# A low-rank gate product run unsplit in four column groups of the array, and a gate product over 128 rows

## The chip, the cores and the metric

The kernel runs on one core of one Trainium2 chip. The metric is device time in microseconds (us) from one execution of the whole program. The core has five engines with an instruction queue each: TensorE (PE in the profile, with its weight loads as PEld), VectorE (DVE), ScalarE (ACT), GpSimd (POOL) and SyncE (SP), which only issues transfers here. Sixteen DMA engines move the data.

## The reference

A two-layer decoder trunk over 256 positions of width 2048. Layer 0 has sliding-window attention heads beside gated linear attention heads; layer 1 has a state-space part beside another gated recurrence. The lines that matter are those of the decay gate of layer 0:

```python
def ab_layer(h, w_in, gla_w_gate, gla_b_gate, gla_norm_g, w_out):      # h is rmsnorm(x) * norm_g
    z = h @ w_in
    qa, ka, va, qb, kb, vb, g_low, gate = jnp.split(z, AB_SPLIT, axis=-1)
    ...
    log_a = jax.nn.log_sigmoid(g_low @ gla_w_gate + gla_b_gate) / GLA_TAU
    ob = chunked_gated_linear_attention(qb * GLA_DK ** -0.5, kb, vb, log_a)
```

`g_low` has 16 columns (the low-rank product, 2048 to 16), and `gla_w_gate` takes these 16 to 512 (the gate product). Inputs and outputs are float32.

## The kernel before, in words

Activations lie feature-major: `hT` holds the input as 16 tiles (`KT`, index `kt`) of 128 features by 256 positions. The norm's factor per position is applied after a product (`rb0`, the same row on all partitions), and its gain per feature (`col(V_NG0 + kt)`) before it, in `split_x`. To keep float32 accuracy at the faster float32r format, the large products are split: `xh` and `xl` are the high and low part of the activations, `wh` (ScalarE, line 168) and `wl` (VectorE, line 169) those of a weight block, and three products are added (lines 181 and 200). Weight blocks come as 1 MB loads `raw` into three buffers, issued on SP (`load_split`). Small products run unsplit in float32.

The order of work: the instructions of an engine run in the order that a planner writes down when the program is built. It takes them by the order of the code, with a model of its own of what an instruction costs and when a result is there; blocks under `urgent()` go first, `issue_after` holds instructions behind a given one, and `hook` inserts prepared pieces between matmuls. Tiles with the same `tag` share a buffer.

What the change touches stands in `trunk`:

- `load_consts`, called with the fourth weight load of the first product, loads constants through SP. `wgt` is the gate weight, 16 rows of 512, loaded twice so that 32 partitions are filled (line 226).
- Lines 368 and 369 split the low-rank weight `glw` (128 by 16 by 16) into `glhl`: its high part in columns 0 to 15, its low part in 16 to 31.
- Lines 370 to 373: for each of the 16 `kt`, the 32 columns of `glhl` times `xh`, and the 16 high columns times `xl`, all into rows 0 to 31 of one PSUM tile `psl`. Rows 0 to 15 end up with the high part's product and rows 16 to 31 with the low part's.
- Line 374 multiplies by `rb0` into `glo`, 32 rows of 256.
- Line 379: four unsplit products of `wgt` (32 rows, 128 columns at a time) with `glo`. The sum over 32 rows adds the two halves. Lines 382 to 387 make the decay `f` from it, which `gla` (line 276) uses later.

Around it stand the transposed norm factor (line 127, just ahead in TensorE's order) and the second weight block's product (line 181). `s5_prep` builds tables for layer 1 from the start on; its transposes at line 935, the transfers of `ed` and `E` and its VectorE work run beside layer 0. `small_blocks` (line 287) and line 308 are unsplit products of 32 and 64 columns inside `gla`, line 504 transposes by a product with the identity, and line 272 clears `AT` (gA in the profile) on GpSimd.

Of the kernel before, what the change touches and what calls it, by code (L numbers as in the profile page):

```python
# [12 lines left out]
F32 = mybir.dt.float32  # L13
F32R = mybir.dt.float32r
I32 = mybir.dt.int32
AF = mybir.ActivationFunctionType
# [4 lines left out]
S = 256  # L21
D = 2048
KT = D // 128
# [4 lines left out]
V_NG0, V_NG1, V_FG, V_BG, V_GN, V_GAM, V_HN, V_BGLU = 0, 16, 32, 48, 52, 60, 76, 84  # L28
# [29 lines left out]
def trunk(ctx: ExitStack, tc: tile.TileContext, I, out):  # L58
    nc = tc.nc
    V, G, A, T = nc.vector, nc.gpsimd, nc.scalar, nc.tensor  # L60
# [16 lines left out]
    hT = xv[:, NV:].rearrange("p (k s) -> p k s", s=S)  # L77
    xh = const.tile([128, KT, S], F32R, name="xh")
    xl = const.tile([128, KT, S], F32R, name="xl")
# [7 lines left out]
    def col(o, n=1):  # L87
        return vec[:, o:o + n]

    def pm_tile(name="pm"):  # L90
        return pm.tile([128, 512], F32, name=name, tag="pm")
# [21 lines left out]
    def finish_norm(tag):  # L113
        V.tensor_add(sqa[:, 0:2], sqa[:, 0:2], sqa[:, 2:4])
        V.tensor_add(sqa[:, 0], sqa[:, 0], sqa[:, 1])
        ps = pm_tile()
        for t in range(2):
            T.matmul(ps[:, t:t + 1], sqa[:, 0, t * 128:(t + 1) * 128], ones[:, 0:1], start=True, stop=True)
        ms = small.tile([128, 2], F32, name="nms")
        V.tensor_scalar(ms, ps[:, 0:2], 1.0 / D, EPS, op0=OP.mult, op1=OP.add)  # L120
        rc = const.tile([128, 2], F32, name=tag + "c")
        rsqrt(rc, ms, 2, "nr")
        pb = pm_tile()
        for t in range(2):
            dg = small.tile([128, 128], F32, name="dg")
            V.tensor_scalar(dg, ident, rc[:, t:t + 1], None, op0=OP.mult)
            T.matmul(pb[:, t * 128:(t + 1) * 128], ones, dg, start=True, stop=True)
        rb = const.tile([128, S], F32, name=tag + "b")
        A.activation(rb, pb[:, 0:S], AF.Copy)
        return rc, rb  # L130
# [12 lines left out]
    def load_split(src, g):  # L143
        raw = stream.tile([128, 4, 512], F32, name="raw", bufs=3)
        first = state["first"]
        state["first"] = first and g < 3
        with urgent():
            if first:
                for a, b in ((0, 1), (1, 2), (2, 3), (3, 4)) if g == 0 else ((0, 2), (2, 4)):
                    xs = slice(NV + (4 * g + a) * S if g + a else 0, NV + (4 * g + b) * S)  # L150
                    load(xv[:, xs], I["xv"][:, xs])
                    for c in (slice(0, 256), slice(256, 512)) if g + a == 0 else (slice(0, 512),):
                        load(raw[:, a:b, c], src[g][:, a:b, c])
                for kt in range(4 * g, 4 * g + 4):
                    split_x(kt, V_NG0)
            else:
                state["load"] = nc.sync.dma_start(raw, src[g])
        if first and g == 3:
            load_consts()
        for half in range(2):  # L160
            wh = stream.tile([128, 2, 512], F32R, name="wh", bufs=3)
            wl = stream.tile([128, 2, 512], F32R, name="wl", bufs=3)
            with urgent():
                for a, b, c, d in (((0, 1, 0, 256), (0, 1, 256, 512), (1, 2, 0, 512)) if first and g == 0
                                   else ((0, 2, 0, 512),)):
                    r = raw[:, 2 * half + a:2 * half + b, c:d]
                    w, l = wh[:, a:b, c:d], wl[:, a:b, c:d]
                    state["wh"] = A.activation(w, r, AF.Copy)  # L168
                    V.tensor_sub(l, r, w)  # L169
            for k in range(2):  # L170
                yield 4 * g + 2 * half + k, wh[:, k], wl[:, k]
            hook()
# [42 lines left out]
    att = ExitStack()  # L215
    ap_ = att.enter_context(tc.tile_pool(name="att", bufs=1))
    glw = mix.tile([128, KT, 16], F32, name="glw", tag="gT1")
    glhl = ap_.tile([128, KT, 32], F32R, name="glhl", tag="pr")
    wgt = ap_.tile([32, 512], F32, name="wgt", tag="qk", bufs=2)
    glo = ap_.tile([32, S], F32, name="glo", tag="qk", bufs=2)  # L220

    def load_consts():
        nc.sync.dma_start(cst, I["cst"])
        nc.sync.dma_start(glw, I["w_low"])
        for n in range(2):
            nc.sync.dma_start(wgt[16 * n:16 * n + 16], I["w_gate"])
        nc.sync.dma_start(msk.rearrange("p a b -> p (a b)"), I["msk"])

    def load(dst, src):
# [16 lines left out]
    rc0, rb0 = finish_norm("r0")  # L246
# [118 lines left out]
            for t in range(2):  # L365
                A.activation(dst[:, t, c0:c0 + 512], ps[:, t], AF.Copy, scale=rc[:, t:t + 1])

    A.activation(glhl[:, :, 0:16], glw, AF.Copy)
    V.tensor_sub(glhl[:, :, 16:32], glw, glhl[:, :, 0:16])
    psl = pm_tile()  # L370
    for kt in range(KT):
        T.matmul(psl[0:32, 0:S], glhl[:, kt], xh[:, kt], start=(kt == 0), stop=False, skip_group_check=True)
        T.matmul(psl[0:16, 0:S], glhl[:, kt, 0:16], xl[:, kt], start=False, stop=(kt == KT - 1), skip_group_check=True)
    V.tensor_mul(glo, psl[0:32, 0:S], rb0[0:32])
    ga = mix.tile([128, 4, S], F32, name="gQ")
    for h0 in range(0, 4, 2):
        ps = pm_tile().rearrange("p (n s) -> p n s", n=2)
# [741 lines left out]
def build(arrays):  # L1119
    nc = bacc.Bacc("TRN2", target_bir_lowering=False, num_devices=1)  # L1120
    I = {k: nc.dram_tensor("in_" + k + "_dram", v.shape, mybir.dt.from_np(v.dtype), kind="ExternalInput").ap()
         for k, v in arrays.items()}
    out = nc.dram_tensor("out_0_dram", (2, 128, D), F32, kind="ExternalOutput").ap()
    with tile.TileContext(nc, schedule_with_timeline_sim=True) as tc:
        trunk(tc, I, out)
    if not nc.is_finalized():
        nc.finalize()
    return nc
# [8 lines left out]
```

## Time and profile before

| | |
|---|---|
| time, median of 3 runs | 893.63 us (893.55 to 894.71) |
| the profiled execution | 892.18 us, span 890.4 us |
| TensorE matmul busy | 874.7 us, 98% |
| VectorE busy | 635.5 us, 71% |
| ScalarE busy | 472.0 us, 53% |
| GpSimd busy | 54.4 us, 6% |
| mean transfer rate | 203 GB/s |
| granted TensorE clock, mean | 0.995 of full speed |

The span is what the profile covers of that execution; its own time is a little longer. Busy times of engines overlap. A row of the timeline or of a tile's view gives start, length, line, operation, the tiles written and read, the shape, and the count.

### The profile page before, as it was taken

To read this page: it belongs to the slowest core of one execution; us is meant where nothing else is said; L and a number is where in the kernel's file an instruction comes from. 1 tells how busy PE (TensorE), PEld (TensorE's weight loads), DVE (VectorE), ACT (ScalarE), POOL (GpSimd) and SP (SyncE) were. 2 spreads that over 40 slices of the span, in tenths; PEclk is the share of its full clock that TensorE was granted. 3 is DMA by queue.
4 is the path that set the end of the run, shared out by engine and by line. 5 is a ranking of instruction groups with operands and counts; after the bars stand their busy time and mean duration, and the time that the engine had idled before them with its cause. 6 is when DMAs were issued, how large, how long until landed. Compare 5 with 4: busy or idle time off the path is not lost.

```text
span 890.4 us, 18689 instructions
## 1 busy us (share of the span) xinstructions
PE 874.7 (98%) x7728; PEld 802.0 (90%) x7728; DVE 635.5 (71%) x1197; ACT 472.0 (53%) x715; POOL 54.4 (6%) x106
## 2 busy tenths in 40 slices
PE   8999999999999999999999999999999999999995
PEld 8987899889998899999999998799877899988894
DVE  7988975989869858756675677676987756665562
ACT  7654546665645765645543335355545475444451
POOL 0001100111101101000000001100110000000000
PEclk9999999999999999999999999999999999999998
DMA  9827743777656555555576566744643544544532
GB/s 317 316 102 218 259 160 146 237 256 251 220 204 230 205 190 196 197 200 199 200 283 222 206 230 198 260 172 167 225 166 139 206 190 172 202 180 177 179 132 94
DMA packets 40388, 180.40 MB, mean 203 GB/s; under 512 B 12720, under 2 KB 14256, under 8 KB 22768
## 3 DMA queue, kind: packets, MB, share of 16 engines
q1 hardware_dynamic: 29440, 154.99, 49.2%
q0 software_dynamic: 7984, 22.69, 7.5%
q10 hardware_dynamic: 2880, 1.54, 0.6%
q8 instruction: 60, 0.98, 0.4%
q14 instruction: 24, 0.20, 0.1%
HBM read 166.48 MB, written 12.71 MB: 201 GB/s over the span
## 4 chain that ended last, share of the span: by engine, by line
PE 81%; DVE 6%; DMA 4%; ACT 4%; issue 3%; SPq 0%; POOL 0%; ACTq 0%; POOLq 0%; DVEq 0%
PE pg L181 47%; PE pg L200 24%; DMA raw<-in_w_dram 2%; PE pg L756 2%; DVE wl L169 2%; PE pm L287 1%; PE pm L339 1%; DMA E<-ed 1%; ACT wh L168 1%; PE pm L621 1%; PE pm L625 1%; PE pm L308 1%; PE pm L415 1%; PE pm L1025 1%; ACT bb L1019 0%
## 5 line engine op out<-in xcount | busy, mean ns | idle before, releaser
L168 ACT ACTIVATE wh<-raw 128x1024 fp32r<-128x1024 f32 (+2 forms) x276 | 287.7, 1046 | 325.4 <-PE pg L181 193.7
L169 DVE TENSOR_TENSOR wl<-raw,wh 128x1024 fp32r<-128x1024 f32 (+2 forms) x276 | 332.0, 1206 | 167.9 <-ACT wh L168 163.1
L181 PE MATMUL pg<-xh,wh 128*128 128x256 f32 x1024 | 161.8, 279 | 2.2 <-ACT wh L168 2.2
L181 PE MATMUL pg<-xh,wl 128*128 128x256 f32 x1024 | 163.2, 280 | 0.4 <-DVE wl L169 0.4
L181 PE MATMUL pg<-xl,wh 128*128 128x256 f32 x1024 | 161.2, 278 | 0.0
L181 PEld LDWEIGHTS pg<-xh,wh 128*128 128x128 f32 x1024 | 136.7, 188 | 3.8 <-ACT wh L168 3.2
L181 PEld LDWEIGHTS pg<-xh,wl 128*128 128x128 f32 x1024 | 137.0, 188 | 1.6 <-DVE wl L169 0.8
L181 PEld LDWEIGHTS pg<-xl,wh 128*128 128x128 f32 x1024 | 136.7, 188 | 0.6 <-issue 0.3
L200 PE MATMUL pg<-wl,xh 128*128 128x512 f32 x320 | 100.9, 396 | 0.6 <-DVE wl L169 0.6
L200 PE MATMUL pg<-wh,xl 128*128 128x512 f32 x320 | 100.7, 394 | 0.0
L200 PE MATMUL pg<-wh,xh 128*128 128x512 f32 x320 | 100.2, 394 | 0.0
L200 PEld LDWEIGHTS pg<-wl,xh 128*128 128x128 f32 x320 | 59.0, 188 | 14.2 <-DVE wl L169 1.4
L200 PEld LDWEIGHTS pg<-wh,xl 128*128 128x128 f32 x320 | 59.8, 188 | 12.8
L200 PEld LDWEIGHTS pg<-wh,xh 128*128 128x128 f32 x320 | 59.3, 188 | 12.8
L181 PE MATMUL pg<-yh,wh 128*128 128x256 f32 x320 | 50.0, 277 | 0.0
L181 PE MATMUL pg<-yl,wh 128*128 128x256 f32 x320 | 49.5, 277 | 0.0
L181 PE MATMUL pg<-yh,wl 128*128 128x256 f32 x320 | 49.5, 277 | 0.0
L181 PEld LDWEIGHTS pg<-yh,wh 128*128 128x128 f32 x320 | 42.6, 188 | 0.0
L181 PEld LDWEIGHTS pg<-yl,wh 128*128 128x128 f32 x320 | 42.4, 188 | 0.0
L181 PEld LDWEIGHTS pg<-yh,wl 128*128 128x128 f32 x320 | 42.4, 188 | 0.0
L965 POOL DMA_DIRECT2D tabs<-pc x44 | 23.8, 547 | 162.3 <-DVE x L975 42.5
L200 PE MATMUL pg<-wh,yh 128*128 128x512 f32 x96 | 30.1, 395 | 0.0
(350 smaller groups left out, 1008.2 us busy)
## 6 DMA issues: line engine op xcount, KB each, us to landing
raw<-in_w_dram SPq DMA_DIRECT2D x100, 1024.0 KB, 4.9
raw<-in_wo_dram SPq DMA_DIRECT2D x28, 1024.0 KB, 4.8
tb<-tabs POOLq DMA_DIRECT2D x8, 768.0 KB, 6.9
tabs<-pc POOLq DMA_DIRECT2D x20, 256.0 KB, 5.5
raw<-in_wg_dram SPq DMA_DIRECT2D x4, 1024.0 KB, 4.8
raw<-in_wo1l_dram SPq DMA_DIRECT2D x4, 1024.0 KB, 4.8
raw<-in_w_dram SPq DMA_DIRECT2D x6, 512.0 KB, 7.9
tabs<-pc POOLq DMA_DIRECT2D x24, 128.0 KB, 4.6
```

Source lines behind the costliest of these rows:

```text
L168: state["wh"] = A.activation(w, r, AF.Copy)
L169: V.tensor_sub(l, r, w)
L181: state["mm"] = T.matmul(ps[:, c], w[:, cs], a[:, kt], start=(i == 0 and n == 0 and c % 2 == 0), stop=(i == last and n == 2), skip_group_c ...
L200: state["mm"] = T.matmul(ps[:, t], a[:, kt, ts_], w, start=(i == 0 and n == 0), stop=(i == last and n == 2), skip_group_check=True)
L287: T.matmul(ps[32 * b:32 * b + 32, t, hd], k[:, hd, r], Q[:, hd, r], start=True, stop=True)
L308: T.matmul(ps[j0:j0 + h, hd, j0 + h:j0 + 2 * h], k[:, hd, b:b + h], Qp[:, hd, b + h:b + 2 * h], start=True, stop=True)
L339: T.matmul(ps[:, (hd - h0) * dv:(hd - h0 + 1) * dv], AT[:, hd, t + j], v[:, j, hd * dv:(hd + 1) * dv], start=(j == 0), stop=(j == t))
L415: T.matmul(ps[:, t, 0:n], q[:, t * 128:(t + 1) * 128], k[:, 0:n], start=True, stop=True)
L621: T.matmul(py[g * 64:g * 64 + 64, pr], w[:, pr], X[:, g, pr], start=(pr == 0), stop=False, skip_group_check=True)
L625: T.matmul(py[gs, pr, 1:64], Pi[gs, pr], t["t"][1][gs, pr, 0:63], start=False, stop=True, skip_group_check=True)
L756: T.matmul(ps[:, t, 0:256], a_[:, kt, ts_], w_, start=(kt == 0 and n == 0), stop=(kt == KT - 1 and n == 2), skip_group_check=True)
L965: nc.gpsimd.dma_start(tabs[qt, dst, n], t[src].rearrange("p a b -> p (a b)"))
```

## The change

The low-rank weight is no longer split. It is multiplied by the norm's gain on VectorE into `glg`, whose columns 16 to 31 are zero (cleared on GpSimd), and multiplied unsplit with `hT` itself. The 16 products go in turn to the four 32-column groups of the array: `kt` 0, 4, 8, 12 add up in rows 0 to 31 of `psl`, `kt` 1, 5, 9, 13 in rows 32 to 63, and so on. Line 374 then spans 128 rows, and the gate product runs over 128 rows, with the gate weight repeated eight times down the partitions, so that its sum adds the four partial products (the rows that belong to the zero columns are zero). The repeated weight comes in one transfer that GpSimd issues, in place of two that SP issued.

```diff
-    glhl = ap_.tile([128, KT, 32], F32R, name="glhl", tag="pr")
-    wgt = ap_.tile([32, 512], F32, name="wgt", tag="qk", bufs=2)
-    glo = ap_.tile([32, S], F32, name="glo", tag="qk", bufs=2)
+    glg = ap_.tile([128, KT, 32], F32, name="glg", tag="pr")
+    wgt = ap_.tile([128, 512], F32, name="wgt", tag="qk", bufs=2)
+    glo = ap_.tile([128, S], F32, name="glo", tag="qk", bufs=2)
...
-        for n in range(2):
-            nc.sync.dma_start(wgt[16 * n:16 * n + 16], I["w_gate"])
+        wg_ = I["w_gate"]
+        nc.gpsimd.dma_start(wgt, bass.AP(tensor=wg_.tensor, offset=wg_.offset, ap=[[0, 8], [512, 16], [1, 512]]))
...
-    A.activation(glhl[:, :, 0:16], glw, AF.Copy)
-    V.tensor_sub(glhl[:, :, 16:32], glw, glhl[:, :, 0:16])
+    G.memset(glg, 0.0)
+    V.tensor_mul(glg[:, :, 0:16], glw, col(V_NG0, KT).unsqueeze(2).to_broadcast([128, KT, 16]))
     psl = pm_tile()
     for kt in range(KT):
-        T.matmul(psl[0:32, 0:S], glhl[:, kt], xh[:, kt], start=(kt == 0), stop=False, skip_group_check=True)
-        T.matmul(psl[0:16, 0:S], glhl[:, kt, 0:16], xl[:, kt], start=False, stop=(kt == KT - 1), skip_group_check=True)
-    V.tensor_mul(glo, psl[0:32, 0:S], rb0[0:32])
+        p = 32 * (kt % 4)
+        T.matmul(psl[p:p + 32, 0:S], glg[:, kt], hT[:, kt], start=(kt < 4), stop=(kt >= KT - 4),
+                 skip_group_check=True)
+    V.tensor_mul(glo, psl[:, 0:S], rb0)
```

## The prediction

> **What bounds the kernel now.** I read four views, in this order: the page's engine shares, what TensorE waited for, the chain that ended last in order of time, and the timeline of TensorE around the lines that change.
>
> ```profile
> span 890.4 us, 18689 instructions
> PE 874.7 (98%) x7728; PEld 802.0 (90%) x7728; DVE 635.5 (71%) x1197; ACT 472.0 (53%) x715; POOL 54.4 (6%) x106
> ```
> ```profile
> PE pg L181 <- ACT wh L168: 2.2, 3, 0.9
> ```
> TensorE (PE) is the bound: 98% busy, and the longest entry of its waits, 2.2 us in three waits, lies in the first 13 us. So 1 us taken out of TensorE's instruction stream should be close to 1 us of the span, as long as what feeds it moves along. The chain, read around the lines of the diff, says the same:
>
> ```profile
> 48.26 0.44 PE pm L127 x4
> 48.70 0.12 PE pm L372
> ...
> 52.35 0.12 PE pm L373
> ...
> 55.29 1.92 PE pm L379 x8
> ...
> 71.38 0.11 PE pm L935
> ```
> The low-rank product (L372 and L373, 16 each) and the gate product (L379) lie on the chain with their whole length. After L935 the chain leaves TensorE for the state-space preparation, but that starts with the transposes at L935, which stand behind all this in TensorE's order; if TensorE arrives there earlier, the transfers and VectorE work behind it start earlier too. I therefore let the full saving pass.
>
> **The change part by part.** First, prices of TensorE work, from the timeline (start, length, line, shape, count; starts are what I use, since the ends overlap).
>
> ```profile
> 48.10 0.60 PE L127 MATMUL pm<-dg,ones 128*128 128x128 f32 x4
> 52.30 0.40 PE L181 MATMUL pg<-xl,wh 128*128 128x256 f32 x2
> 54.42 0.64 PE L181 MATMUL pg<-xh,wh 128*128 128x256 f32 x4
> 54.90 0.40 PE L181 MATMUL pg<-xl,wh 128*128 128x256 f32 x2
> 55.22 1.99 PE L379 MATMUL pm<-glo,wgt 32*128 32x256 f32 x8
> 57.14 0.51 PE L181 MATMUL pg<-xl,wh 128*128 128x256 f32 x2
> 57.49 0.62 PE L181 MATMUL pg<-xh,wl 128*128 128x256 f32 x4
> 121.09 0.28 PE L181 MATMUL pg<-xh,wl 128*128 128x256 f32 x1
> 121.30 0.76 PE L287 MATMUL pm<-gQ,gk 128*32 128x32 f32 x64
> 121.99 0.62 PE L181 MATMUL pg<-xh,wl 128*128 128x256 f32 x3
> 122.45 0.62 PE L181 MATMUL pg<-xh,wh 128*128 128x256 f32 x4
> 136.65 0.28 PE L181 MATMUL pg<-xh,wh 128*128 128x256 f32 x1
> 136.85 1.15 PE L308 MATMUL pm<-gQ,gk 128*64 128x64 f32 x16
> 137.93 0.62 PE L181 MATMUL pg<-xh,wh 128*128 128x256 f32 x3
> 741.48 1.91 PE L504 MATMUL pm<-cst,gz 128*128 128x128 f32 x16
> 743.14 0.72 PE L181 MATMUL pg<-xh,wh 128*128 128x256 f32 x4
> ```
> What the reader is to see: an unsplit float32 matmul shows as two records (L379 issues 4 in the code and has 8 here), a split one (float32r) as one. A float32 record of 128 columns takes (743.14 - 741.48)/16 = 0.104 us, so one of 256 columns about 0.21 us, near the 0.24 us of L379, which includes a changeover. A split record of 256 columns at L181 takes (54.90 - 54.42)/4 = 0.12 us.
>
> (1) Old low-rank product. L127's four records start at 48.10 and need 4 x 0.107, so the product begins at 48.53; the next L181 starts at 52.30. It costs 3.77 us for 32 records.
>
> (2) New low-rank product: 16 unsplit matmuls of 256 columns, 32 records. One after the other that is 32 x 0.214 = 6.85 us, more than before. All depends on whether four column groups run at once. L287 has the same form: 128 rows, 32 columns, unsplit, four neighbouring matmuls into the four 32-partition strips of one tile. From the end of the L181 before (121.09 + 0.114) to the next L181 is 0.79 us; the three L181 after it take 0.46 instead of 0.34, so it costs 0.91 us in all for 64 records. Serially, 64 records of 32 columns would need 64 x 0.104/4 = 1.66 us. So they overlap; with four at a time the records need 16 rounds of 0.026 to 0.032, or 0.42 to 0.51, and the other 0.40 to 0.49 is the changeover into and out of the narrow shape. The 64-column L308, 16 records on one strip and so serial, costs 137.93 - 136.76 + 0.12 = 1.29 us, of which 16 x 0.052 to 0.058 is work: again about 0.4 for the changeover. New price: 8 rounds x 0.214 + 0.40 = 2.11 us. Saving 3.77 - 2.11 = 1.66 us. Accumulation over kt stays inside a group (kt and kt + 4 hit the same strip), so it adds no wait between groups.
>
> (3) Gate product. Now it uses 32 rows: L181 before it would end at 55.14, the next starts at 57.14, and the first two of those take 0.35 instead of 0.235: 2.12 us for 8 records, 0.4 more than 8 x 0.214. With 128 rows it is a full-array matmul as at L504, where 16 records of 128 columns cost 1.76 us all told, changeover included; 8 of 256 columns are the same work: 1.71 to 1.76. Saving 0.36 to 0.41, taken 0.38.
>
> (4) VectorE and ScalarE.
>
> ```profile
> L368 ACT ACTIVATE glhl<-glw x1: 398/398/398, 25.9 to 25.9; 128x256 fp32r<-128x256 f32 x1
> L369 DVE TENSOR_TENSOR glhl<-glw,glhl x1: 415/415/415, 27.4 to 27.4; 128x256 fp32r<-128x256 f32 x1
> L374 DVE TENSOR_TENSOR glo<-pm,r0b x1: 411/411/411, 52.6 to 52.6; 32x256 f32<-32x256 f32 x1
> L226 SPq DMA_DIRECT2D wgt<-in_w_gate_dram x2: 315/328/340, 16.4 to 17.7; - x2
> ```
> The ScalarE copy (0.40) goes; ScalarE was waiting on VectorE around it, so I count nothing. The subtraction at L369 becomes a multiplication over the same 256 elements a partition, 0.41 for 0.41. L374 spans 128 partitions instead of 32, with the same 256 elements each: the same 0.41 (if it doubled, the 2.2 us between its end at 53.0 and L379 at 55.22 still covers it).
>
> (5) GpSimd and the transfer of wgt. Two SP issues of 32 KB go; one GpSimd transfer writes 128 rows of 2 KB, 256 KB, so 192 KB more. GpSimd gets that issue and a 128x512 memset.
>
> ```profile
> 0.88 1.38 POOL L272 MEMSET gA<- 128x1536 f32 x1
> ```
> ```profile
> 0.00:5.00 5.00, 3.98 (x16) 3.56 (x16) 1.72 (x14) 2.60 (x6) 1.76 (x7) 1.00 0.55 153
> 5.00:14.00 9.00, 6.87 (x54) 6.39 (x54) 7.15 (x28) 6.42 (x14) 0.00 (x0) 1.00 0.97 340
> 14.00:31.00 17.00, 16.72 (x145) 16.41 (x144) 16.55 (x51) 14.25 (x20) 0.00 (x0) 1.00 1.02 389
> ```
> ```profile
> 11.87 8.94 DMA raw<-in_w_dram
> ...
> 29.97 1.14 DVE wl L169
> 31.15 9.12 PE pg L181 x78
> ```
> The memset is 512/1536 of 1.38 = 0.46 us on an idle engine; gA behind it is first written by ScalarE past 120 us, so nothing waits. The transfer is different. It depends on nothing, so GpSimd, which has nothing to do before gA's memset at 0.88 us, can issue it at about 1 us, and it joins the start, where the DMA share (second last column) is 0.97 and 1.02 from 5 to 31 us and the chain runs through a weight load that took 8.94 us to land. 192 KB at the 389 GB/s of that stretch is 0.51 us, all 256 KB ahead of the first loads 0.67. Against that, the first 5 us have a share of only 0.55, which can take part of it. Bounds 0 and 0.7 us; I take 0.3, nearer the lower end because of the free share early and the 64 KB that leave the busy stretch. The two SP issues saved are worth nothing while SP waits for landings.
>
> Sum: -1.66 - 0.38 + 0.30 = -1.74 us. The profiled execution took 892.18 us (span 890.4, some 1.8 around it), 1.45 below the median 893.63 of the runs. So about 890.4 for an execution like the profiled one, and 891.9 against the median: 0.19% less. From no change I count only what exceeds 0.2%, 1.8 us, about what a measurement of this kernel can tell. My forecast sits on that edge.
>
> **The rivals.**
> Two at a time: the two records of one matmul stand next to each other in the same group. If a record may not start before the one ahead of it has, only the second half of one matmul and the first half of the next overlap: 17 rounds of 0.214 + 0.4 = 4.04 us in place of 3.77, and with the 0.38 and 0.3 the time is 893.8, no change. Against it: L287, under that rule, needs at least 33 x 0.026 + 0.4 = 1.26 us and cost 0.91. For it: that is 32 columns, this is 256. The Trainium skill, "TensorE: Matmul & The Clock Gate", section "Part 3: Packing small matmuls", calls matmuls "strict FIFO, no reordering" in start and end; taken literally that is this rival, and the L287 row speaks against it. The same section gives a speedup of 2.38 for three column tiles at 512 columns; as an estimate from that page, 79% of the ideal would make the 1.71 us 2.16 and the time 892.3.
>
> No overlap at 256 columns (the other side): if four streams of long moving data cannot be fed together, the product costs 6.85 + 0.4 = 7.25 us, 3.48 more; minus 0.38, plus 0.3: 897.0, slower. It decides from 5.7 us for the product on, i.e. below 1.3 records at a time. Only L287's 32-column moving data speaks against it, but over 64 records in a row.
>
> Another order: the instruction order on each engine comes from a planner with its own costs; other costs for the product shift everything it places later. If L379 moves up right behind the product, TensorE waits for L374 (0.28 us after the last record, 0.41 long): about 0.7 us, 892.6. If VectorE's multiplication is placed ahead of glw's landing near 24 us, wl at 29.97 and so TensorE at 31.15 slip by up to 2 us: 893.9. A luckier order could put L935 earlier and give 1 to 2 us: 890.5. Nothing in the profile of before tells which.
>
> The start pays in full (0.7 us instead of 0.3): 892.3.
>
> **How the numbers follow.** Four groups overlap and the order stays about as it is: 0.62, of which 0.36 falls below 891.84 and 0.26 above. Two at a time 0.08 (same). No overlap 0.05 (slower). Another order 0.17: 0.09 faster, 0.08 slower. Full price at the start or a VectorE stall 0.08 (same). Together faster 0.45, same 0.42, slower 0.13. The likeliest case alone spans 890.9 (start free, full saving) to 892.6. The range 889.6 to 895.2 takes in both signs of another order and two at a time, and leaves out no overlap and the tails.
>
> **What would show it.** Right: the product's 32 unsplit records lie within about 2.1 us from first record to next L181, and L379's within 1.8 with 128 rows; L935 starts about 1.7 us earlier than 71.38. Wrong at step 2: 3.5 us or 7 us there. Wrong at step 5: the first gap-free L181 after 13 us and the one at 31.15 come more than 0.7 us later, or not at all later. Wrong on passing the saving on: L935 early, but TensorE's waits between 75 and 130 us grow by as much as was saved.

## The result, and the profile after

The changed kernel is slower: 900.25 us median (898.3 to 904.4), against 894.5 us for the kernel before on the same chip. The ratio is 1.0063, 95% interval 1.0049 to 1.0077, some 5.7 us. I had forecast 891.9. One profile further down (e9) comes from an execution with a granted clock of 0.85 from 10 us on; its times are set beside others only after scaling.

The page of the changed kernel, the same two lines as before, and what TensorE waited for (engine, tile, line, releaser: us in total, times, longest). Lines behind 372 have moved by one or more against the kernel before: the product is L373, the gate product L380, the evacuation of the first product L391.

```profile
span 897.7 us, 18689 instructions
PE 879.9 (98%) x7728; PEld 804.7 (90%) x7728; DVE 636.3 (71%) x1197; ACT 471.9 (53%) x714; POOL 55.4 (6%) x108
```
```profile
PE pg L181 <- ACT wh L168: 4.5, 2, 2.4
```
In the two profiled executions the span grew by 7.3 us, TensorE's busy time by 5.2 and the waits at L181 by 2.3. The two products are not among the losers. TensorE's timeline around them:

```profile
55.18 0.61 PE L127 MATMUL pm<-dg,ones 128*128 128x128 f32 x4
55.72 1.93 PE L373 MATMUL pm<-xv,glg 128*32 128x256 f32 x32
57.58 0.74 PE L181 MATMUL pg<-xh,wl 128*128 128x256 f32 x4
58.16 0.64 PE L181 MATMUL pg<-xh,wh 128*128 128x256 f32 x4
...
60.04 0.64 PE L181 MATMUL pg<-xl,wh 128*128 128x256 f32 x4
60.52 1.89 PE L380 MATMUL pm<-glo,wgt 128*128 128x256 f32 x8
62.05 0.82 PE L181 MATMUL pg<-xh,wl 128*128 128x256 f32 x4
62.71 0.62 PE L200 MATMUL pg<-wh,xh 128*128 128x512 f32 x2
```
By the prediction's way of reading: L127 is over at 55.18 + 4 x 0.107 = 55.61, the next L181 starts at 57.58 and its four records take 0.58 instead of 0.47, so the product costs 2.08 us (forecast 2.11). Record by record, the trace shows eight rounds of four records: the four start within 21 ns of one another, and the next round 0.22 us later. The gate product costs 62.05 - 60.51 + 0.19 = 1.73 us (forecast 1.71 to 1.76). But L127 itself starts 7.1 us later than before's 48.10; 1.6 of that is fourteen L181 that the order now puts ahead of it. The loss lies elsewhere.

To see where, I counted the matmuls of L181 and L200, which are the same 5,280 in every kernel here (at most 44 of them change places), and compared the start of the n-th with its start before, both from the start of the span. The columns are named by the start before; the last is the last of these matmuls. Each row comes from one execution.

| start before, us | 24.28 | 33.09 | 59.30 | 93.77 | 124.27 | 345.42 | 595.56 | 855.14 |
|---|---|---|---|---|---|---|---|---|
| changed kernel, us later | 1.5 | 5.4 | 3.4 | 6.5 | 5.6 | 5.5 | 6.0 | 7.1 |

Four things happen before 125 us, and a fifth behind. First, at the start. The waits in TensorE's timeline of the kernel before, then TensorE and ScalarE of the changed kernel, then its transfer (instruction times in ns, then first and last start in us):

```profile
5.28 0.51 PE L181 MATMUL pg<-xh,wh 128*128 128x256 f32 x2 [0.30 <-ACT wh L168]
...
7.63 0.74 PE L181 MATMUL pg<-xh,wh 128*128 128x256 f32 x4 [0.94 <-ACT wh L168]
...
12.92 0.73 PE L181 MATMUL pg<-xh,wh 128*128 128x256 f32 x4 [0.92 <-ACT wh L168]
```

```profile
7.21 0.50 PE L181 MATMUL pg<-xh,wh 128*128 128x256 f32 x2 [2.42 <-ACT wh L168]
...
9.43 1.22 PE L181 MATMUL pg<-xh,wh 128*128 128x256 f32 x4
10.45 0.94 PE L181 MATMUL pg<-xl,wh 128*128 128x256 f32 x4
```
```profile
6.74 0.42 ACT L168 ACTIVATE wh<-raw 128x256 fp32r<-128x256 f32 x1 [2.40 <-DMA raw<-in_w_dram]
```
```profile
L226 POOL DMA_DIRECT2D wgt<-in_w_gate_dram x1: 814/814/814, 1.3 to 1.3; - x1
```
The second piece of the first weight load lands at 6.72 us, where before it landed at 4.79, and GpSimd's 256 KB, issued at 1.3 us, at 6.96; TensorE waits 2.42 us where before it waited 0.30; before's two later waits, 0.94 and 0.92, are gone in return. After that four matmuls take 1.02 us (10.45 - 9.43) instead of 0.46: the granted clock fell. The windows show it (stretch, PE, PEld, DVE, ACT, POOL, then the clock; 1.00 before in both):

```profile
0.00:14.00 14.00, 10.49 (x58) 9.76 (x59) 8.15 (x44) 8.07 (x17) 3.16 (x9) 0.88 0.81 268
31.00:48.00 17.00, 14.88 (x114) 14.48 (x112) 13.30 (x46) 9.05 (x9) 0.00 (x0) 0.90 0.49 167
```
Second, at 31 us. ScalarE's timeline of the kernel before, and then of the changed one:

```profile
28.30 1.99 ACT L168 ACTIVATE wh<-raw 128x1024 fp32r<-128x1024 f32 x2
30.20 1.00 ACT L390 ACTIVATE gq<-pg 128x1024 f32<-128x1024 f32 x1
```
```profile
31.68 1.02 ACT L391 ACTIVATE gq<-pg 128x1024 f32<-128x1024 f32 x1 [2.51 <-PE pg L181]
32.60 2.00 ACT L168 ACTIVATE wh<-raw 128x1024 fp32r<-128x1024 f32 x2
```
The planner has put the evacuation of the first product ahead of two halves of the second weight block. That evacuation waits for TensorE's last matmul of the first product, and TensorE then waits for the halves behind it:

```profile
33.70 0.74 PE L181 MATMUL pg<-xh,wh 128*128 128x256 f32 x4 [2.06 <-ACT wh L168]
34.28 0.62 PE L181 MATMUL pg<-xl,wh 128*128 128x256 f32 x4
34.96 1.22 PE L181 MATMUL pg<-xh,wl 128*128 128x256 f32 x4
35.98 1.06 PE L181 MATMUL pg<-xh,wh 128*128 128x256 f32 x4
36.83 1.06 PE L181 MATMUL pg<-xl,wh 128*128 128x256 f32 x4
37.69 0.96 PE L181 MATMUL pg<-xh,wl 128*128 128x256 f32 x4
38.49 0.63 PE L181 MATMUL pg<-xh,wh 128*128 128x256 f32 x4
```
The wait costs 2.06 us, and from 34.96 to 38.49 sixteen matmuls take 3.53 us instead of 4 x 0.46: 1.7 more, 3.8 in all. That is the step from 1.5 to 5.4. The Trainium skill, "TensorE: Matmul & The Clock Gate", section "Part 1: The HAM clock gate", has the clock at half rate after an idle window of about 3.4 us. The half-speed stretch here is about that long (3.5 us); the wait ahead of it was 2.06 us, so a much shorter pause than a whole window already cost the clock. It doesn't always: e5 waits 3.00 us here and goes on at full pace (rows at the end).

Third, the two products give back 2.0 us (5.4 to 3.4). Fourth, the small blocks of the first recurrence (L287) are scattered: up to the end of the second set of 64 they stand in 13 pieces instead of 6 between the large matmuls. One of them:

```profile
78.37 0.63 PE L200 MATMUL pg<-wh,xl 128*128 128x512 f32 x2
78.93 0.32 PE L287 MATMUL pm<-gq,gk 128*32 128x32 f32 x12
79.17 0.74 PE L200 MATMUL pg<-wl,xh 128*128 128x512 f32 x2
79.75 0.62 PE L200 MATMUL pg<-wh,xh 128*128 128x512 f32 x2
```
From the end of the L200 before (78.37 + 0.46) to the next is 0.34 us, and the next pair takes 0.58 instead of 0.46: 0.46 us, of which the twelve records' work is 0.08 to 0.10. Each piece pays the changeover of about 0.4 us that the prediction read from whole sets, and seven pieces more come to about 3 us. (The pieces are counted in TensorE's timeline: the first starts at 69.48 and the thirteenth at 112.60, before at 71.41 and the sixth at 105.65.)

The account up to 125 us: +1.5 (start) + 3.8 (order on ScalarE) - 2.0 (the products) + 3 (pieces) - 0.8 (between 94 and 124 us; 0.3 of it is a wait of before at L287 that is gone, the rest stays open) = +5.5.

Fifth, 1.0 of the 1.5 us that come behind 125 us is neither a wait nor another order of TensorE in that place. Windows of the kernel before, then of the changed kernel (stretch, TensorE's busy time and matmuls, granted clock, DMA):

```profile
750.00:785.00 35.00, 35.00 (x311) 1.00 0.57 206
```
```profile
750.00:785.00 35.00, 35.00 (x299) 1.00 0.48 176
```
TensorE does nothing but L181 there, in the same sequence, without a wait and at a granted clock of 1.00, and yet it goes at 0.113 us per matmul before and at 0.118 after the change. Every trace has stretches at the one pace and stretches at the other, and within an uncut stretch the pace doesn't change; a cut of 0.13 us can be enough for a change (e1 at 367.81 us). What sets it isn't shown. The kernel before, e5, e6 and e14 have the quick pace in this place; the changed kernel and all the others but e9 have the slow one and lose 1.0 us by it. In e1 and e4 a longer stretch is slow too (681 and 682 matmuls from 370 to 450 us, 708 before): 4 us of what their rows lose between 345 and 596 us are this pace.

### The profile page after: what moved, and what is told of

It is laid out like the page before. It is cut to its first block, busy times and chain, and to the rows that moved or that the text cites. A ratio compares the mean times of both kernels' runs of the same rounds, so it can differ in the third digit from the quotient of the medians.

```text
span 897.7 us, 18689 instructions
## 1 busy us (share of the span) xinstructions
PE 879.9 (98%) x7728; PEld 804.7 (90%) x7728; DVE 636.3 (71%) x1197; ACT 471.9 (53%) x714; POOL 55.4 (6%) x108
## 4 chain that ended last, share of the span: by engine, by line
PE 86%; DVE 5%; issue 3%; ACT 2%; DMA 2%; ACTq 0%; SPq 0%; POOL 0%; POOLq 0%; DVEq 0%
PE pg L181 50%; PE pg L200 25%; PE pg L757 2%; DVE wl L169 1%; PE pm L287 1%; PE pm L339 1%; PE pm L622 1%; PE pm L626 1%; PE pm L584 1%; DMA raw<-in_w_dram 1%; PE pm L308 1%; ACT wh L168 1%; PE pm L1026 1%; DMA s5y<-ys 1%; DMA yc<-s5y 1%
## 5 line engine op out<-in xcount | busy, mean ns | idle before, releaser
L181 PE MATMUL pg<-xh,wh 128*128 128x256 f32 x1024 | 163.2, 281 | 4.6 <-ACT wh L168 4.5
L181 PE MATMUL pg<-xh,wl 128*128 128x256 f32 x1024 | 165.6, 283 | 0.1
L181 PE MATMUL pg<-xl,wh 128*128 128x256 f32 x1024 | 162.8, 280 | 0.0
L181 PEld LDWEIGHTS pg<-xh,wh 128*128 128x128 f32 x1024 | 138.0, 190 | 6.4 <-ACT wh L168 5.7
L181 PEld LDWEIGHTS pg<-xh,wl 128*128 128x128 f32 x1024 | 139.2, 190 | 1.5 <-issue 0.4
L181 PEld LDWEIGHTS pg<-xl,wh 128*128 128x128 f32 x1024 | 138.4, 190 | 0.2
L200 PE MATMUL pg<-wl,xh 128*128 128x512 f32 x320 | 101.7, 398 | 0.6 <-DVE wl L169 0.6
L200 PE MATMUL pg<-wh,xl 128*128 128x512 f32 x320 | 101.1, 395 | 0.0
L200 PE MATMUL pg<-wh,xh 128*128 128x512 f32 x320 | 100.7, 395 | 0.0
L200 PEld LDWEIGHTS pg<-wl,xh 128*128 128x128 f32 x320 | 58.7, 188 | 14.3 <-DVE wl L169 1.9
L200 PEld LDWEIGHTS pg<-wh,xl 128*128 128x128 f32 x320 | 59.8, 188 | 12.8
L200 PEld LDWEIGHTS pg<-wh,xh 128*128 128x128 f32 x320 | 59.2, 188 | 12.7
L181 PE MATMUL pg<-yh,wh 128*128 128x256 f32 x320 | 49.9, 277 | 0.0
L181 PE MATMUL pg<-yl,wh 128*128 128x256 f32 x320 | 49.5, 277 | 0.0
L181 PE MATMUL pg<-yh,wl 128*128 128x256 f32 x320 | 49.4, 277 | 0.0
L181 PEld LDWEIGHTS pg<-yh,wh 128*128 128x128 f32 x320 | 42.4, 188 | 0.0
L181 PEld LDWEIGHTS pg<-yl,wh 128*128 128x128 f32 x320 | 42.3, 188 | 0.0
L181 PEld LDWEIGHTS pg<-yh,wl 128*128 128x128 f32 x320 | 42.3, 188 | 0.0
L200 PE MATMUL pg<-wh,yh 128*128 128x512 f32 x96 | 30.1, 394 | 0.0
```

What stands on the lines that cost most here:

```text
L181: state["mm"] = T.matmul(ps[:, c], w[:, cs], a[:, kt], start=(i == 0 and n == 0 and c % 2 == 0), stop=(i == last and n == 2), skip_group_c ...
L200: state["mm"] = T.matmul(ps[:, t], a[:, kt, ts_], w, start=(i == 0 and n == 0), stop=(i == last and n == 2), skip_group_check=True)
```

## The experiments

Theory A: the products save what was forecast; the transfer at the start and, above all, another order of the instructions that the change doesn't touch cost more. Rivals: the products cost more than they save further on; the transfer is all of it; the order is worth little. Columns as in the table above; "ratio" is against the kernel before, with its interval.

| kernel | ratio | 24.28 | 33.09 | 59.30 | 93.77 | 124.27 | 345.42 | 595.56 | 855.14 |
|---|---|---|---|---|---|---|---|---|---|
| e1 evacuation held | 1.0065 [1.0042, 1.0089] | 1.1 | 1.7 | -0.3 | 5.2 | 4.7 | 5.5 | 9.7 | 10.8 |
| e2 blocks held | 1.0043 [1.0027, 1.0060] | 1.4 | 4.7 | 3.1 | 5.6 | 4.3 | 3.9 | 3.7 | 5.5 |
| e3 both held | 1.0046 [1.0030, 1.0063] | 1.8 | 2.0 | 0.1 | 4.4 | 3.1 | 4.1 | 4.0 | 5.8 |
| e4 both, transfer on SP | 1.0048 [1.0030, 1.0067] | 0.2 | 3.9 | 2.1 | 2.3 | 2.1 | 6.6 | 10.5 | 12.2 |
| e5 transfer alone | 1.0192 [1.0157, 1.0226] | 2.4 | 5.7 | 6.1 | 16.2 | 15.6 | 15.1 | 15.4 | 15.5 |
| e6 products alone | 1.0024 [1.0006, 1.0041] | -0.1 | 1.5 | -0.7 | -1.5 | -0.2 | 3.9 | 4.2 | 4.2 |
| e7 before, blocks held | 1.0028 [1.0007, 1.0048] | 0.8 | 0.3 | 0.3 | -1.0 | 0.8 | 2.3 | 2.2 | 4.0 |
| e8 products, blocks held | 1.0013 [0.9995, 1.0030] | 0.6 | 1.0 | -1.1 | -2.4 | 0.4 | 0.7 | 1.8 | 3.5 |
| e10 transfer held | 1.0119 [1.0083, 1.0155] | -0.1 | 4.2 | 2.4 | 13.0 | 12.0 | 11.7 | 12.0 | 13.1 |
| e11 eight loads | 0.9989 [0.9969, 1.0009] | 0.1 | 0.3 | -1.1 | -2.0 | -0.8 | 2.6 | 2.6 | 3.7 |
| e12 copies on VectorE | 1.0038 [1.0014, 1.0061] | -0.1 | 1.4 | -2.4 | -1.1 | 0.8 | 3.6 | 3.6 | 4.7 |
| e13 eight loads, blocks held | 1.0013 [0.9994, 1.0033] | 0.0 | -0.1 | -2.3 | -3.5 | -2.9 | -0.9 | -1.0 | 1.0 |
| e14 eight loads, late | 1.0054 [1.0033, 1.0075] | -0.3 | -0.1 | -5.9 | 1.7 | 1.7 | 4.2 | 4.2 | 4.2 |
| e15 late, blocks held | 1.0050 [1.0030, 1.0071] | 0.9 | 1.6 | -4.4 | 1.6 | 1.7 | 2.4 | 2.4 | 4.2 |

(In e14 and e15 the two products stand behind the matmul of the column 59.30, so that column leaves their cost out. The ratio is from medians, a row from one execution: e4's took 904.37 us, the longest of its eleven, against a median of 898.79.)

**e1 to e4: repair one place after another in the changed kernel.** e1 holds the evacuation behind the halves, e2 holds the small blocks behind the last large matmul ahead of them, e3 does both, e4 also issues the 128-row transfer on SP.

```diff
 e1, e3, e4
-    with urgent():
-        A.activation(q, psq, AF.Copy, scale=128 ** -0.5)
+    def evac_q():
+        with tc.issue_after(state["wh"].ins), urgent():
+            A.activation(q, psq, AF.Copy, scale=128 ** -0.5)
+
+    fillq.extend([[], [evac_q]])
 e2, e3, e4 (behind = state["mm"].ins, taken at the start of gla)
+            with tc.issue_after(behind):
...
                 T.matmul(ps[32 * b:32 * b + 32, t, hd], k[:, hd, r], Q[:, hd, r], start=True, stop=True)
 e4
-        nc.gpsimd.dma_start(wgt, ...)
+        nc.sync.dma_start(wgt, ...)
```


> The changed kernel, with the evacuation of q (line 391) held on ScalarE behind the two wh copies of the second weight block, as it stood before the change; nothing is left out. Theory A (ScalarE order): the 2.06 us wait of TensorE at 31.65 us and the half clock after it (together +3.75 us in the profile of the changed kernel) go, so the time falls by 3 to 4 us against the changed kernel, to about 1.002 to 1.003 of before. Rival B (the wgt transfer at the start holds back everything that follows, and the wait at 31.65 only shows it): the wait comes back elsewhere before 48 us and the time stays at 1.005 to 1.006 of before.

> The changed kernel, with the small products of line 287 held on TensorE behind the last matmul of the weight block ahead of them, so that they run in whole blocks of 64 records and more and not in pieces; nothing is left out. Theory A (pieces): each piece costs about 0.43 us of changeover, 13 pieces become one, about 3 us at line 200 between 60 and 113 us go; some of it comes back as a wait for VectorE (0.8 us in before), so 2 to 3 us less than the changed kernel, about 1.003 to 1.004 of before. Rival (the pieces fill time in which TensorE would wait anyway): no gain against the changed kernel, 1.006, and a wait of 2 us or more at line 287.

> Both of the two above in the changed kernel. Theory A: the two losses lie in different places and add up, 5 to 7 us less than the changed kernel, 0.9985 to 1.0005 of before; left against before are the start (+1.2 to 1.5 us) and the gain of the two products (-2.0 us). Rival B (start): 1.003 to 1.006.

> As the one before, with the 256 KB transfer of wgt issued by SP at its old place among the constants and not by GpSimd at 1.3 us. Theory A: TensorE's wait of 2.42 us at 7.21 us goes back to what it was before the change, the start is 1 to 1.5 us shorter, and the time is 0.9965 to 0.9990 of before. Rival (192 KB more in a full stretch of transfers cost about 0.5 us wherever they are issued): no difference from the kernel with GpSimd's transfer beyond 0.5 us.

e2 came out about as expected (1.0043 for 1.003 to 1.004); e1, e3 and e4 did not. In e1 the step at 31 us is gone (1.1 to 1.7 in place of 1.5 to 5.4), and a new wait takes its place. VectorE's and TensorE's timelines of e1:

```profile
82.03 0.69 DVE L978 TENSOR_TENSOR pc<-E,pB 128x512 f32<-128x512 f32 x1 [5.36 <-DMA E<-ed]
```
```profile
85.93 0.73 PE L200 MATMUL pg<-wl,xh 128*128 128x512 f32 x2 [2.57 <-DVE wl L169]
```
VectorE stands 5.36 us at the first product with E, a table of layer 1 that isn't there yet, and the wl halves are queued behind it. The kernel before has this wait too, 3.55 us at 87.70, but TensorE's matmuls go on beside it. In e3 VectorE waits 5.60 us and TensorE 3.78 behind it. e4 has the start repaired (0.2 at 24.28) but loses 3.7 us at 31 us after all: with the evacuation behind the halves, TensorE still waits 2.09 us for them at 32.18, because one more instruction of the norm (L110) now stands ahead of them on ScalarE, and waits 1.29 us for VectorE. In the whole e4 is no better than e3. Mending one place makes the planner write another order with another wait.

The wait for E is in every kernel here, from 3.28 us in the changed kernel to 8.75 in e10. Where VectorE stands 4.9 us or longer (e1, e3, e5, e8, e10, e12, e14, e15), TensorE stands 1.6 to 6.0 us behind it; where it stands less, TensorE stands at most 1.1, with one exception (e2, 3.30 and 1.94).

The hold of e2 has a second effect. `gla` is called again in layer 1, and its blocks are held there too: TensorE waits 1.25 to 1.51 us at one of them, between 665 and 678 us, in all seven kernels with the hold, and the pieces that the hold saves there give back only a part of it: each is 0.6 to 0.9 us later behind that place.

**e5 and e6: the two halves of the change, each alone.** e5 is the kernel before with the 128-row transfer on GpSimd and the old products, which use 32 of its rows. e6 has the new products with the weight loaded as before.

```diff
 e5, against the kernel before
-    wgt = ap_.tile([32, 512], F32, name="wgt", tag="qk", bufs=2)
+    wgt = ap_.tile([128, 512], F32, name="wgt", tag="qk", bufs=2)
...
-        for n in range(2):
-            nc.sync.dma_start(wgt[16 * n:16 * n + 16], I["w_gate"])
+        nc.gpsimd.dma_start(wgt, ...)          # 128 rows
 e6, against the changed kernel
-        nc.gpsimd.dma_start(wgt, ...)
+        for n in range(2):
+            nc.sync.dma_start(wgt[16 * n:16 * n + 16], I["w_gate"])
...
     G.memset(glg, 0.0)
+    for p in range(32, 128, 32):
+        G.tensor_copy(wgt[p:p + 32], wgt[0:32])
```


> The kernel before with one part of the change alone: wgt is 128 rows, loaded by GpSimd's one transfer of 256 KB; the products stay split and the gate product reads its first 32 rows. Theory C (the transfer is the loss, directly at the start and through the order that the planner then writes): TensorE loses 1.2 to 1.5 us by 16 us as in the changed kernel; the planner's order now has the evacuation of q ahead of eight wh copies on ScalarE and the first product with E behind 23 instead of 31 wl on VectorE, so 3 us or more are lost between 30 and 110 us; 1.005 to 1.010 of before. Rival D (the other cost that the planner sees in the unsplit product makes the order bad): 1.0 to 1.002 here.

> The changed kernel without its transfer: wgt comes in the two 32 KB transfers of before, and GpSimd, idle at that time, copies its 32 rows three times down the partitions. Both products are the new ones. Theory C: the start and ScalarE's order are those of before (32 instead of 31 wl ahead of the first product with E), the low-rank product costs 2.1 to 2.2 us for 3.8 and the gate product 1.75 for 2.13, so 1 to 2.5 us less than before, 0.997 to 0.999. Rival D: 1.003 or more.

e5 is the clearest single result: the transfer alone costs 1.9%, three times what the whole change costs. Only a small part of it is at the start (2.4 us at 24.28). Ten more us come between 59 and 94 us. It is the wait for E again: the first of its rows below is VectorE's first product with E, whose second transfer landed at 75.42 us, and VectorE makes what the small blocks need (gQ) and the wl halves behind it. The rows of VectorE, then of TensorE:

```profile
75.50 0.69 DVE L974 TENSOR_TENSOR pc<-E,pB 128x512 f32<-128x512 f32 x1 [5.15 <-issue]
...
77.91 1.22 DVE L279 TENSOR_TENSOR gQ<-gq,gf 128x1024 f32<-128x1024 f32 x1
```
```profile
79.28 0.54 PE L287 MATMUL pm<-gQ,gk 128*32 128x32 f32 x20 [3.53 <-DVE gQ L279]
81.02 1.22 PE L200 MATMUL pg<-wl,xh 128*128 128x512 f32 x2 [1.21 <-DVE wl L169]
```
e6 has an undisturbed start, and its products cost what they do in the changed kernel. It is 1.5 us ahead of before at 93.77 and still 0.2 ahead at 124.27, then loses 4.1 us in the attention stage up to 345.42, 200 us behind the products. TensorE's waits between 200 and 345 us make up about half of that: 0.9 for VectorE's wl, 0.7 at L434 and 0.5 at L438, where before has 0.4 in all. Neither expectation was met: e5 is worse, e6 worse than 0.999.

**e7 and e8: the held blocks of e2 in the kernel before and in e6.**

> The kernel before with the small products of line 287 held in whole blocks. The six pieces of before cost about 0.43 us each, five of them go: 2.1 us, some of which comes back as waits at line 287; 0.998 to 1.0.

> The products alone (small transfers, copies on GpSimd) with the small products of line 287 in whole blocks; the order on the engines is nearly that of the kernel before with whole blocks. Theory C: 1.5 to 2.2 us less than that kernel, 0.9955 to 0.998 of before. Rival D: no less than that kernel.

e7 does the work of the kernel before and nothing else, in another order, and is 0.28% slower. So another order is worth as much as the whole gain that I had forecast, though 1.0 of e7's 4.0 us at the end is the slow pace and not the order. With the products e8 is 0.15% below e7 (expected: 1.5 to 2.2 us, 0.17 to 0.25%), in the direction of theory A but within the intervals.

**e9: the four groups in turn.** The instructions of e6 in the same order on every engine; only the group of a block differs. An unsplit record of the gate product took 0.245 us in its profile and 0.216 in e6's.

```diff
-        p = 32 * (kt % 4)
-        T.matmul(psl[p:p + 32, 0:S], glg[:, kt], hT[:, kt], start=(kt < 4), stop=(kt >= KT - 4),
+        p = 32 * (kt // 4)
+        T.matmul(psl[p:p + 32, 0:S], glg[:, kt], hT[:, kt], start=(kt % 4 == 0), stop=(kt % 4 == 3),
```


> The products of the change alone (e6), with one expression altered: the sixteen blocks of the low-rank product go to the four column groups in turn, four blocks to group 0, then four to group 1 and so on, instead of a new group with every block. The instructions and their order on every engine are those of e6. Theory A (step 2 of the prediction: records run side by side only when they stand in different groups next to one another): the 32 records of 0.214 us run nearly one after another, 6.2 to 6.9 us instead of 1.7, so PE is 4.5 to 5.1 us later behind the product; if PE stays the bound from there on, the whole is 0.4 to 0.55% above e6's 1.0024, 1.0065 to 1.008. Rival: the four groups are not what made it short (a record of 32 columns is cheap by itself); then the product stays at 1.7 us and the ratio at 1.002. Second rival: the waits behind the product swallow it; the product takes 6.5 us and the ratio stays below 1.005.

TensorE's timeline of e6 and then of e9:

```profile
50.15 1.93 PE L375 MATMUL pm<-xv,glg 128*32 128x256 f32 x32
52.01 0.50 PE L181 MATMUL pg<-xl,wh 128*128 128x256 f32 x2
```
```profile
51.62 5.13 PE L375 MATMUL pm<-xv,glg 128*32 128x256 f32 x32
56.68 0.53 PE L181 MATMUL pg<-xl,wh 128*128 128x256 f32 x2
```
The product takes 1.86 us in e6 and 5.06 in e9, which at e6's pace (0.216 / 0.245) is some 4.5. That the neighbouring records stand in different groups is what makes the product short: the first rival falls. It is less than the 6.2 to 6.9 that I had worked out from full-width records, so records of different groups overlapped even here. The starts of the single records show how: there are twenty rounds of about 0.245 us, and in twelve of them two records start within 28 ns. The first of these pairs comes with the fifth record, and the weight load ahead of it waits for the same input block as that of the fifth matmul in e6: the second group has begun while the first has only half its eight records behind it. The whole is 1.0044 [1.0016, 1.0071] against e6's 1.0024 [1.0006, 1.0041]: 0.2% for 2.6 us (0.29%), which agrees with passing on in full, but by the intervals with none of it too.

**e10: the transfer held back** behind the last input block, in the changed kernel.

```diff
+        G.tensor_copy(wgt[0:1, 0:1], hT[0:1, 15, 0:1])
         nc.gpsimd.dma_start(wgt, ...)
```


> The changed kernel with its 256 KB transfer held back on GpSimd: a copy of one element from the last input block into the tile stands ahead of the transfer, so that it can't start before that block has landed, at some 14 us instead of 1.3 us. Theory A (the transfer in front of the first weight loads costs 1.5 to 2.5 us at the start, the rest of the loss is the order that the planner wrote): the granted clock of the first 14 us is 1.00 again and the main matmuls of the first 14 us are within 0.3 us of before; the evacuation of the first product still stands ahead of the wh halves on ScalarE and the small blocks still come in 13 pieces, so the whole is at 1.0035 to 1.006. Rival D (the transfer's bytes cost nothing, all is order): the start is no better than in the changed kernel and the ratio is 1.006 or more. Rival E (the start is all of it): 0.999 to 1.001.

The transfer starts at 21.8 us (I had expected 14), since the copy ahead of it sat idle for 18.6 us until the last input block had landed. The windows of e10:

```profile
0.00:14.00 14.00, 12.50 (x70) 11.59 (x70) 9.10 (x42) 9.08 (x19) 2.22 (x8) 1.00 0.83 273
31.00:48.00 17.00, 15.25 (x116) 15.10 (x117) 16.05 (x63) 7.95 (x8) 0.00 (x0) 0.90 0.58 219
```
The start is before's again to 0.1 us, with the clock at 1.00. So the loss at the start is the transfer's, and this part of theory A holds. The ratio is a miss all the same: 1.0119. VectorE's and TensorE's timelines show the same E, 8.75 us this time (the row names no releaser, but E's second transfer landed at 79.84 us):

```profile
79.92 0.69 DVE L976 TENSOR_TENSOR pc<-E,pB 128x512 f32<-128x512 f32 x1 [8.75 <-issue]
```
```profile
83.84 0.79 PE L200 MATMUL pg<-wl,xh 128*128 128x512 f32 x1 [6.02 <-DVE wl L169]
```

**e11 and e12: the weight brought in by other means.** e11 loads it eight times on SP and needs no copies; e12 is e6 with the three copies on VectorE.

```diff
 e11, against e6
-        for n in range(2):
+        for n in range(8):
             nc.sync.dma_start(wgt[16 * n:16 * n + 16], I["w_gate"])
...
-    for p in range(32, 128, 32):
-        G.tensor_copy(wgt[p:p + 32], wgt[0:32])
 e12, against e6
-        G.tensor_copy(wgt[p:p + 32], wgt[0:32])
+        V.tensor_copy(wgt[p:p + 32], wgt[0:32])
```


> The products of the change, the gate weights' eight copies loaded by eight transfers of 32 KB on SP, where before has two, and nothing on GpSimd. The small blocks come in 4 pieces (13 in the changed kernel, 6 before) and the evacuation of the first product stands behind the wh halves. Theory A: what the transfer on GpSimd and the scattered blocks cost is gone, the two products give their 2 us by 120 us, and what the attention stage does with it isn't known: 0.998 to 1.003. Rival (the products themselves cost more than they save): 1.004 or more, with PE no earlier than before at 120 us.

> The products of the change, the gate weights loaded as before and copied to the other three groups by VectorE instead of GpSimd. The three copies add some 0.4 us each to VectorE and give the planner another order once more: the small blocks come in 6 pieces, with 8 wh halves behind the evacuation. Theory A (the products save 2 us, an order costs or gives 1 to 4 us by itself): 0.998 to 1.004, and other than e6 and e11 by more than their intervals in at least one of the three. Rival (the order is worth little, e6 and e8 were slow for the products' sake): all three agree with e6's 1.0024 within 0.1%.

e11 is the best of all: 0.9989 [0.9969, 1.0009], no different from before and 0.74% below the changed kernel, from which only the way the weight is loaded differs. Its start is untouched, and it is 2.0 us ahead at 93.77: what the two products were forecast to save. e6, e11 and e12 do the same products and lie from 0.9989 to 1.0038, so the rival that an order is worth little falls.

**e13 to e15: does the gain reach the end in some order?** e13 is e11 with e2's held blocks. e14 wraps the code from `psl = pm_tile()` to the last activation on `f` into a function that `fillq` issues inside the key product; e15 does that to e6 and holds the blocks too.

> e11 (the products of the change, the gate weights' copies by eight transfers on SP) with the small blocks of the first recurrence held behind the last matmul of the query, key and value products, as in e2, e7 and e8. e7, which has the old products and the same held blocks, stood at 1.0028; e8, with the new ones and e6's start, at 1.0013; e11 lost 0.9 us less at the start than e6. Theory A (the products give 2 us wherever the order lets them): 1 us below e8 and 2 to 2.5 us below e7, 0.998 to 1.0005, with PE 0.5 to 1.5 us ahead of before at 150 us. Rival (the products' gain is always taken back by a wait behind them): 1.001 to 1.003, as e7 and e8.

> e11 with the low-rank and the gate products written down later in the program, as fillers of the key product, so that the planner numbers them behind the second weight load: another order with the same instructions. In the attention stage fewer instructions stand elsewhere than in before (16 matmuls where e11 has 64 in the first part of it). Theory A (order alone decides the sum of 1 to 4 us between these kernels): PE ahead of before by 1 us or more at 150 us, and a loss between 178 and 345 us that is other than e11's 3.4 us; 0.997 to 1.003. Rival (that loss comes from the products, not the order): again 3 to 4 us between 178 and 345 us.

> The products of the change written down later as in e14, the gate weights by the two transfers of before and GpSimd copies as in e6, the small blocks held as in e8: of the orders written so far the one that is nearest to before's between 50 and 200 us (50 matmuls stand elsewhere, e8 has 471). Theory A: 0.997 to 1.001, 1 to 3 us below e8 by 150 us if the order is what e8 lacked. Rival: 1.001 to 1.003, as e6 and e8.

e13 is further ahead at 124 us, 2.9, than theory A asked for (0.5 to 1.5 at 150 us; the blocks in one piece give the rest). The first evacuation of `gA` on ScalarE, one instruction that every kernel has, says it in rows of the timelines of before, the changed kernel and e13:

```profile
144.13 0.60 ACT L318 ACTIVATE gA<-pm 128x512 f32<-128x512 f32 x1
```
```profile
149.67 0.60 ACT L318 ACTIVATE gA<-pm 128x512 f32<-128x512 f32 x1
```
```profile
141.31 0.60 ACT L320 ACTIVATE gA<-pm 128x512 f32<-128x512 f32 x1
```
Two of these 2.9 us are lost between 205 and 345 us, and two more behind 595 us (0.9 with the blocks held in layer 1, 1.0 by the slow pace of 741 to 787 us); the profiled span ends 0.9 us behind that of before. The only TensorE waits left between 200 and 345 us in e13 are 0.9 at L434 and 0.8 at L200; before has 0.4 there. e14 and e15, with the gate chain later, get the wait for E again (VectorE 5.30 and 5.51 us, TensorE 1.82 and 1.91 behind it) and stand at 1.0054 and 1.0050, both outside what I had expected.

No version here beats the kernel before by more than its interval. An order that keeps e13's 2.9 us to the end was not found, and whether there is one stays open.

## Why the prediction was wrong

Steps 1 to 3 held: the product costs 2.08 us (2.11 forecast), in eight rounds of four records as forecast, the gate product 1.73 (1.71 to 1.76), and e9 shows that the four groups make the difference. "Two at a time" (4.04 us) and "no overlap" are out; so is the literal reading of "strict FIFO" in the Trainium skill, "TensorE: Matmul & The Clock Gate", section "Part 3: Packing small matmuls", by which the product would have cost 4.04.

Step 4, VectorE and ScalarE at nothing, was right for the durations (0.41 and 0.43 us for the multiplications) and blind to their places in the order.

Step 5 was mis-sized. I had priced the transfer by its bytes, 0 to 0.7 us, and taken 0.3. It cost 1.5 us at 24 us (2.4 in e5; 0.1 or less where it is away or held, in e6, e10 and e11), because the one small load that TensorE was waiting for landed 1.9 us later beside it, and the wait then took the clock. The test that I had named for it (more than 0.7 us later) is met.

The step that failed is "four groups overlap and the order stays about as it is", 0.62 of the chance. The order did not stay, in this kernel or in any of the others that ran, and what it cost, 3.8 us on ScalarE and 3 us in pieces, is larger than every term of the sum. The rival "another order" was there with 0.17, but with at most 2 us for a wait and without the clock that falls after it. "Full saving let pass" failed with it: e6, e11 and e13 carry 1.5 to 3.5 us to 94 us and lose it, e6 and e11 partly by 124 us and the rest in the attention stage, e13 there and behind. Half of the loss in the attention stage is waits of TensorE for VectorE and ScalarE; the rest stays open. No term of the sum, and none of my theories, held the two paces of L181, worth 1.0 us here.

One bound doesn't follow from its terms: the likeliest case with a free start and the full saving is 893.63 - 1.66 - 0.41 = 891.6, not 890.9.

## What to carry to other kernels

Where a planner writes the order, an edit's price is the price of its instructions plus that of a new order. Here what came beside the work itself lay between about 1 and 17 us whatever the edit was, so compare the queues' order first, and try the edit in several forms that load the same data by other means: e11 and the changed kernel differ by 0.74% for that alone. Never send bulk that nobody needs soon ahead of the loads that the first matmuls wait for. A wait of some 2 us on TensorE can cost nearly twice its length, so enter both prices. And before a difference of 1 us is explained by an order, compare the pace of the matmuls that run without a wait.

## What the hardware showed that I had not expected

- The clock fell to half for about 3.4 us after a single wait of 2.06 us (0.90 over 31 to 48 us) and after one of 2.42 (0.88 over the first 14 us), while the waits of 0.94 and 0.92 in the kernel before left it at 1.00. In the first 850 us of all traces but e9's, 16 of TensorE's 18 waits of 1.8 to 6.0 us led to a stretch at half pace, and none of the six between 1.3 and 1.6 did. The two that didn't are 1.91 us in e15 and the one in e5:

```profile
35.27 0.74 PE L181 MATMUL pg<-xh,wh 128*128 128x256 f32 x4 [3.00 <-ACT wh L168]
...
37.38 0.64 PE L181 MATMUL pg<-xh,wh 128*128 128x256 f32 x4
37.85 0.64 PE L181 MATMUL pg<-xl,wh 128*128 128x256 f32 x4
```
- 32 unsplit records of 256 columns in four groups ran in 1.86 us from the first to the next matmul, though the two records of one matmul belong to the same group; in turn they took some 4.5, and a later group's records began before an earlier group's were through.
- L181 runs at 0.113 or 0.118 us per matmul, at the same granted clock of 1.00, for stretches of up to 100 us.
- A load of 128 KB landed 1.9 us later beside a transfer of 256 KB issued at 1.3 us, in a stretch where the transfer engines were busy for only 0.55 of the first 5 us before.
